# Where the prompt's top-k rounds are written: one block ahead of the mixer loop, or shared out inside it

## The chip, the core and the metric

The kernel runs on one core of a Trainium2 chip. The metric is the device time of one execution in microseconds (us): 992.89 us is the median of three runs of the kernel before (992.37 to 999.76).

## What is computed

One inference step of a decoder layer, for 512 new prompt tokens and for 8 sequences of 4 new tokens each (32 "sample" tokens) that attend to 1024 cached positions in pages. Two attention branches work on the same normalised input:

```
# branch A: an index score picks 256 keys per query, then softmax attention over those
score = einsum('bth,bths->bts', w_i, relu(einsum('bthe,bse->bths', q_i, k_i))) * (IDX_DIM ** -0.5)
_, idx = lax.top_k(where(causal, score, -inf), n_sel)        # n_sel = 128 for the prompt, 256 for the samples
o_a = softmax(q_a . k_a[idx]) @ v_a[idx]
# branch B: stick-breaking attention, exp(log_beta + later) from a reversed cumulative sum
merged = gates[0] * (o_a @ w_br_a) + gates[1] * (o_b @ w_br_b)
h = x + merged @ w_o
y = rmsnorm(h + ffn(rmsnorm(h)))                              # SwiGLU feed-forward, width 2816
```

The new key and value rows are outputs too. All is float32.

## The kernel before

**Matrix products.** A float32 weight is split into a rounded high part (`wh`, on ScalarE, L113) and a low part (`wl`, on GpSimd, L117), the activations likewise (`xh`, `xl`), and each product is three TensorE passes (`xh·wh`, `xh·wl`, `xl·wh`, L502). These passes are most of TensorE's work. They are called dense rows below.

**Stages, in the program's order.** Normalising the input; the index projections (`dense_idx`), then the index scores of prompt and samples (`idx_prompt`, `idx_sample`); the projections of branch B (`dense_qb`, `dense_kb`, `dense_vb`); then the top-k of the prompt; then the mixer loop (`beside`); then merging, the output projection, the feed-forward network and the final norm.

**The two top-k.** `topk_prompt` (L658 to L662) works on three score tiles of 256, 384 and 512 columns, one for each block of 128 queries after the first. For each it makes 16 rounds (L619, L620): VectorE finds the eight largest values of each row, and replaces them by a mark; at the end L662 makes the mask from the marks. That is 48 rounds and three closing instructions, all on VectorE. `topk_sample` (L624 to L657) finds each sample query's 256th largest score by bisection over the 32 bits of a float: per bit VectorE counts the scores above a candidate (L632), TensorE adds the counts of four partition groups by a product with a 128x128 matrix and one column (L635), and VectorE reads that sum and forms the next candidate (L636, then L641; L639 and L643 at the first and last bit). Its scores come by four small transfers of the SP queue (L627). When the bits are done, VectorE makes the mask `mask_s` in seven instructions (L648 to L656).

**The mixer loop.** `beside` draws three generators in turn: `samples` (branch B, then branch A, for the samples), `heads` (branch B for the prompt: L859, L935, L938 to L942, L866, L875; then branch A for the prompt: L859, L972 to L976, L866, L875) and a chain of dense work (gates, branch A's projections, then branch B's output product). Before each draw `topk_share` (L1331) draws from `topk` until `TK_N` times the progress of the stream is reached. The last uses: the prompt's masks are read at L972, the samples' mask at L1145 by a product that starts the sample scores of branch A.

**What sets the order.** The program is built with a scheduler that replays the program in its own timeline and decides each engine's order; the order in which Python emits the instructions is its input and not its result. Each engine then runs its list strictly in turn: an instruction that waits holds back all behind it on that engine.

**Buffers that matter here.** The score products of branch A and B for the prompt (L859) write one pair of PSUM banks, `z`, of which there is a single buffer: the next L859 waits until the last reader of the pair is done (L942 in branch B, L972 in branch A).

Of the kernel before, what the change touches and what calls it, by code (L numbers as in the profile page):

```python
# [279 lines left out]
def chain(gens):  # L280
    for g in gens:
        yield from g
# [3 lines left out]
S_COST = 130  # L286
H_COST = 80
D_COST = 174
TK_N = 80
D_LAT = 6.0  # L290
G_LAT = 8.0
H_LAG = 1
# [7 lines left out]
def hybrid_step(ctx: ExitStack, tc: tile.TileContext, x_prompt, x_sample, cache_kv_a, cache_k_idx, cache_kv_b,  # L300
# [315 lines left out]
    def rounds(w, m, count):  # L616
        for _ in range(count):
            m8 = cpool.tile([P, 8], F32, tag="m8", name="m8", bufs=4)
            nc.vector.max(out=m8[:m], in_=w)  # L619
            nc.vector.match_replace(out=w, in_to_replace=m8[:m], in_values=w, imm_value=TAKEN)  # L620
            yield 0

    def topk_sample():


        for g in range(4):
            nc.sync.dma_start(score4[g * NS:(g + 1) * NS, :], score_s[:, g * part:(g + 1) * part])  # L627
        cand = cpool.tile([P, 1], I32, tag="cand", name="cand", bufs=3)
        nc.gpsimd.memset(cand, 0)
        for bit in range(31, -1, -1):  # L630
            cnt = cpool.tile([P, 1], F16, tag="cnt", name="cnt", bufs=2)
            nc.vector.tensor_scalar(ge4, score4, cand.bitcast(F32), None, op0=OP.is_ge, op1=OP.add, accum_out=cnt)  # L632
            ps = lat()
            ps, flip = ps[:, :1], ps[:, 1:2].bitcast(I32)
            nc.tensor.matmul(ps, group, cnt, start=True, stop=True)  # L635
            nc.vector.tensor_scalar(flip, ps, float(NSEL), -1.0 if bit == 31 else float(1 << bit), op0=OP.is_lt, op1=OP.mult)  # L636
            new = cpool.tile([P, 1], I32, tag="cand", name="cand", bufs=3)
            if bit == 31:
                nc.vector.tensor_scalar(new, flip, 1 << 30, None, op0=OP.bitwise_xor)  # L639
            elif bit:  # L640
                nc.vector.scalar_tensor_tensor(new, flip, 1 << (bit - 1), cand, op0=OP.bitwise_xor, op1=OP.bitwise_xor)  # L641
            else:
                nc.vector.tensor_tensor(new, flip, cand, op=OP.bitwise_xor)  # L643
            cand = new
            yield 0
        least, rank_s = cand[:NS].bitcast(F32), mask_s.bitcast(F16)
        more = cpool.tile([NS, 2], F32, name="more")
        nc.vector.tensor_scalar(tied_s, score_s, least, None, op0=OP.is_equal)  # L648
        nc.vector.tensor_scalar(score_s, score_s, least, None, op0=OP.is_gt, op1=OP.add, accum_out=more[:, 0:1])
        nc.vector.tensor_scalar(more[:, 1:2], more[:, 0:1], -1.0, float(NSEL), op0=OP.mult, op1=OP.add)  # L650
        nc.vector.tensor_tensor_scan(rank_s, tied_s, tied_s, 0.0, OP.add, OP.bypass)
        nc.vector.scalar_tensor_tensor(tied_s, rank_s, more[:, 1:2], tied_s, op0=OP.is_le, op1=OP.mult)
        nc.vector.tensor_add(score_s, score_s, tied_s)
        nc.vector.tensor_scalar(mask_s[:, :PAST].rearrange("q (j k) -> q k j", j=8),
                                score_s[:, :PAST].rearrange("q (k j) -> q k j", j=8), -NEG, NEG, op0=OP.mult, op1=OP.add)
        nc.vector.tensor_scalar(mask_s[:, PAST:], score_s[:, PAST:], -NEG, NEG, op0=OP.mult, op1=OP.add)  # L656
        yield 0  # L657

    def topk_prompt():
        for i in (1, 2, 3):  # L660
            yield from rounds(work_p[i - 1], P, 16)
            nc.vector.tensor_scalar(mask_p[i - 1], work_p[i - 1], -3.2e38, -NEG, op0=OP.is_gt, op1=OP.mult)  # L662
# [582 lines left out]
    V["hp"] = hp  # L1245
    for _ in chain([dense_qb(), dense_kb(), dense_vb()]):
        pass
    for _ in topk_prompt():
        pass
    topk = topk_sample()  # L1250

    V["wide"], V["banks"] = False, cycle([mm, acc])

# [76 lines left out]
    def topk_share(share):  # L1330
        while done[0] < TK_N * share:  # L1331
            next(topk, None)
            done[0] += 1
# [463 lines left out]
```

## Time and profile before

| what | us |
|---|---|
| median of three runs | 992.89 |
| the profiled execution | 993.59 |
| its span, first to last instruction | 991.8 |
| TensorE busy in the span | 936.3 |
| VectorE busy | 642.0 |
| first prompt round (L619) to the last, start | 86.6 to 163.7 |
| first sample bit (L632) to the last, start | 177.8 to 363.9 |
| first use of the samples' mask (L1145) | 404.1 |

The mixer loop runs from about 175 us to 517 us of the span. A row of the profile that names a group gives the line, the engine, the operation, output<-input, shapes and count, then busy time, mean duration in ns, and the idle time of that engine just before with what ended it. A row of the timeline begins with the start and the duration in us; what stands in brackets at its end is the time its engine stood idle before it and what released it. A row of the windows gives the stretch, its length, and for each engine the busy time and the number of instructions, then TensorE's granted clock as a share of full speed, and the DMA share.

### The profile page before, as it was taken

To read this page: it belongs to the slowest core of one execution; us is meant where nothing else is said; L and a number is where in the kernel's file an instruction comes from. 1 tells how busy PE (TensorE), PEld (TensorE's weight loads), DVE (VectorE), ACT (ScalarE), POOL (GpSimd) and SP (SyncE) were. 2 spreads that over 40 slices of the span, in tenths; PEclk is the share of its full clock that TensorE was granted. 3 is DMA by queue.
4 is the path that set the end of the run, shared out by engine and by line. 5 is a ranking of instruction groups with operands and counts; after the bars stand their busy time and mean duration, and the time that the engine had idled before them with its cause. 6 is when DMAs were issued, how large, how long until landed. Compare 5 with 4: busy or idle time off the path is not lost. (4 is left out here: it accounts for less than half of the span.)

```text
span 991.8 us, 19649 instructions
## 1 busy us (share of the span) xinstructions
PE 936.3 (94%) x7412; PEld 846.0 (85%) x7412; DVE 642.0 (65%) x1238; ACT 450.0 (45%) x889; POOL 301.0 (30%) x260
## 2 busy tenths in 40 slices
PE   5989999889898999999989999999999999999995
PEld 4989999756476885778778999989999999999994
DVE  4466998465464657543405576987778788875874
ACT  6224543445244444544565446444444445442453
POOL 3633353211221221313257356122322322201331
PEclk9989999989998999999998999999999999999998
DMA  9773554967786488516376744123333431235212
GB/s 267 188 190 108 142 147 135 296 190 213 241 258 209 135 294 289 178 55 224 110 230 211 215 131 129 44 80 91 87 107 98 115 97 30 67 94 162 81 49 91
DMA packets 180409, 150.67 MB, mean 152 GB/s; under 512 B 12379, under 2 KB 147355, under 8 KB 179291
## 3 DMA queue, kind: packets, MB, share of 16 engines
q1 hardware_dynamic: 175146, 134.45, 45.6%
q0 software_dynamic: 1872, 10.75, 3.0%
q10 hardware_dynamic: 3296, 4.23, 1.4%
q8 instruction: 58, 0.95, 0.4%
q14 instruction: 37, 0.30, 0.1%
HBM read 126.43 MB, written 17.56 MB: 145 GB/s over the span
## 5 line engine op out<-in xcount | busy, mean ns | idle before, releaser
L117 POOL TENSOR_TENSOR wl<-wst,wh 128x512 fp32r<-128x512 f32 (+2 forms) x136 | 161.2, 1207 | 305.7 <-ACT wh L113 298.3
L502 PE MATMUL mm<-xh,wh 128*128 128x256 f32 (+2 forms) x464 | 141.4, 305 | 7.7 <-ACT hT L1381 5.5
L502 PE MATMUL mm<-xl,wh 128*128 128x256 f32 (+2 forms) x464 | 137.9, 297 | 0.1
L502 PE MATMUL mm<-xh,wl 128*128 128x256 f32 (+2 forms) x464 | 136.9, 295 | 0.1
L237 POOL TENSOR_TENSOR wl<-wst,wh 128x512 fp32r<-128x512 f32 (+1 forms) x48 | 68.7, 1453 | 171.9 <-ACT wh L234 156.6
L502 PEld LDWEIGHTS mm<-xh,wh 128*128 128x128 f32 (+1 forms) x464 | 89.3, 192 | 19.0 <-ACT hT L1381 5.7
L113 ACT ACTIVATE wh<-wst 128x1024 fp32r<-128x1024 f32 (+3 forms) x83 | 75.1, 906 | 52.8 <-PE ts L1647 20.5
L502 PEld LDWEIGHTS mm<-xl,wh 128*128 128x128 f32 (+1 forms) x464 | 89.1, 192 | 5.4 <-issue 4.5
L234 ACT ACTIVATE wh<-ws 128x1024 fp32r<-128x1024 f32 (+1 forms) x55 | 54.9, 998 | 80.2 <-PE ffB L1562 29.2
L502 PEld LDWEIGHTS mm<-xh,wl 128*128 128x128 f32 (+1 forms) x464 | 89.1, 192 | 1.9 <-issue 1.4
L239 DVE TENSOR_TENSOR wl<-ws,wh 128x1024 fp32r<-128x1024 f32 (+1 forms) x55 | 66.6, 1211 | 6.2 <-ACT wh L234 6.2
L234 ACT ACTIVATE wh<-wst 128x1024 fp32r<-128x1024 f32 (+1 forms) x34 | 34.8, 1024 | 21.4 <-PE ffB L1562 14.7
L1030 PE MATMUL ts<-ident,kb 128*128 128x128 f32 x256 | 40.0, 286 | 2.3 <-PE ts L1030 0.7
L237 POOL TENSOR_TENSOR wl<-raw,wh 128x384 fp32r<-128x384 f32 x14 | 15.0, 1088 | 79.5 <-ACT wh L234 64.4
L941 DVE TENSOR_TENSOR_SCAN g<-g,z 128x128 f32<-128x128 f32 (+3 forms) x32 | 26.1, 817 | 19.7 <-ACT z L939 16.9
L538 ACT ACTIVATE rowy<-mm 128x256 f32<-128x256 f32 (+1 forms) x40 | 15.7, 393 | 49.0 <-PE mm L502 40.4
L1030 PEld LDWEIGHTS ts<-ident,kb 128*128 128x128 f32 x256 | 29.7, 145 | 9.4 <-ACT kk L843 2.0
L938 ACT ACTIVATE g<-z 128x128 f32<-128x128 f32 (+3 forms) x32 | 13.9, 436 | 49.8 <-PE z L935 35.9
L843 ACT ACTIVATE kk<-ts 128x512 f32<-128x512 f32 x43 | 25.1, 598 | 21.5 <-PE ts L1030 20.9
L1647 PE MATMUL ts<-actp,wh 128*128 128x288 f32 x160 | 34.1, 295 | 0.0
L211 DVE TENSOR_TENSOR ws<-wst 128x1024 f32<-128x1024 f32 (+1 forms) x11 | 19.7, 1790 | 19.6 <-DMA wst<-in_w_ffn_up 19.0
L1740 PE MATMUL dnB<-x,wh 128*128 128x272 f32 x144 | 29.8, 291 | 0.0
(486 smaller groups left out, 3099.2 us busy)
## 6 DMA issues: line engine op xcount, KB each, us to landing
wst<-in_w_in SPq DMA_DIRECT2D x38, 512.0 KB
kb<-in_cache_kv_b SPq DMA_DIRECT2D x64, 256.0 KB
vb<-in_cache_kv_b SPq DMA_DIRECT2D x64, 256.0 KB
wst<-in_w_ffn_gate SPq DMA_DIRECT2D x40, 256.0 KB
wst<-in_w_ffn_up SPq DMA_DIRECT2D x40, 256.0 KB
wst<-in_w_ffn_down SPq DMA_DIRECT2D x16, 320.0 KB
gate_d<-rowy SPq DMA_DIRECT2D x16, 272.0 KB
gt<-gate_d SPq DMA_DIRECT2D x16, 272.0 KB
```

The source lines that it names most:

```text
L113: self.nc.scalar.activation(h, st, AF.Copy)
L117: self.nc.gpsimd.tensor_sub(l[:, k], st[:, k], h[:, k].bitcast(F32))
L211: v.tensor_add(t, a("A21"), a("A22"))
L234: self.nc.scalar.activation(h, src, AF.Copy)
L237: self.nc.gpsimd.tensor_sub(l[:, g], src[:, g], h[:, g].bitcast(F32))
L239: self.nc.vector.tensor_sub(l, src, h.bitcast(F32))
L502: nc.tensor.matmul(ps, ww[:, k, :m], aa[:, k, hs], start=(k == 0 and p == 0), stop=(k == nk - 1 and p == 2))
L843: nc.scalar.activation(dst, ps, AF.Copy)
L941: nc.vector.tensor_tensor_scan(gr, gr, z[:, :n], 1.0, OP.mult, OP.bypass)
L1030: nc.tensor.transpose(tp[:, (2 * j + pg) * P:(2 * j + pg + 1) * P], raws[pg][:, (2 * jj + j) * P:(2 * jj + j + 1) * P], ident)
L1647: nc.tensor.matmul(ps, ww[:, k - ks[0], :], aa[:, hs], start=(k + p == 0), stop=(k + 1 == DOWN[-1][-1] and p == 2))
L1740: nc.tensor.matmul(ps, ww[:, k, :], t[:, i, :], start=(first and k == 0 and p == 0), stop=(k == KQ - 1 and p == 2), skip_group_check=True)
```

## The change

The prompt's rounds are no longer drawn to their end ahead of the loop; they are put in front of the samples' bisection in the generator that the loop draws from, and the number of draws over the loop's progress rises from 80 to 200. The generator now has 48 + 33 draws instead of 33, so that both versions have emitted the last of them at about two fifths of the loop.

```
-TK_N = 80
+TK_N = 200
...
     for _ in chain([dense_qb(), dense_kb(), dense_vb()]):
         pass
-    for _ in topk_prompt():
-        pass
-    topk = topk_sample()
+    topk = chain([topk_prompt(), topk_sample()])
```

No instruction is added or removed: each engine has the same instructions as before. What differs is the order that the scheduler makes of them, and it differs only inside the mixer loop. The first 203 rows of VectorE's list are the same in both versions, and all 96 rows of the prompt's rounds are among them; at the loop's end the last 419 rows are the same again. TensorE's list is the same in its first 1068 and its last 3232 rows.

First place: VectorE at the start of the loop. `g` and `b` are branch B's tiles, L845 is a copy out of PSUM, `ge`, `cnt` and `cand` belong to the samples' bisection. Before:

```order
L620 MATCH_REPLACE work_263<-m_1993,work_263 128x512
L806 TENSOR_TENSOR rlin<-rlin,wrow 32x256
L799 TENSOR_REDUCE sTi<-rli 128x8x4 x2
L662 TENSOR_SCALAR work_263<-work_263 128x512
L807 TENSOR_REDUCE sTi<-rlin 32x32
L817 TENSOR_TENSOR score_s<-tp,masks 32x32
L845 COPY kk<-ts 128x512
L1016 COPY qb<-qsm 64x8x4 x8
L632 TENSOR_SCALAR ge_266,cnt<-score_265,cand 128x264
L1074 TENSOR_TENSOR zr<-acc,masks 128x32
L636 TENSOR_SCALAR tp<-tp 128x1
L941 SCALAR_TENSOR_TENSOR g_2040<-g_2040,z 128x128
```

Now:

```order
L620 MATCH_REPLACE work_263<-m_3606,work_263 128x512
L806 TENSOR_TENSOR rlin<-rlin,wrow 32x256
L799 TENSOR_REDUCE sTi<-rli 128x8x4 x2
L662 TENSOR_SCALAR work_263<-work_263 128x512
L807 TENSOR_REDUCE sTi<-rlin 32x32
L817 TENSOR_TENSOR score_s<-tp,masks 32x32
L845 COPY kk<-ts 128x512
L1016 COPY qb<-qsm 64x8x4 x8
L1074 TENSOR_TENSOR zr<-acc,masks 128x32
L941 SCALAR_TENSOR_TENSOR g_1893<-g_1893,z 128x128
L942 TENSOR_TENSOR b<-z,g_1893 128x128
L845 COPY kk<-ts 128x512
```

The prompt's last round (L620) and closing instruction (L662) stand where they stood; what left this place is the samples' bisection. Its first count (L632) is now 20 rows later, its first sum on TensorE (L635) 435 rows later, in the middle of branch B, and its last sum 257 rows later (row 2109 instead of 1852).

Second place: VectorE at the end of the bisection, where `mask_s` is made; `sm` and `mx` are branch A's softmax tiles for the prompt. Before:

```order
L651 SCALAR_TENSOR_TENSOR mask_s<-tied_s 32x1056
L650 TENSOR_SCALAR more<-more 32x1
L652 SCALAR_TENSOR_TENSOR tied_s<-mask_s,more,tied_s 32x1056
L972 ISA sm,mx<-z,masks 128x128
L972 ISA mx 128x1
L972 ISA sm,mx<-z,masks 128x128
L972 ISA mx 128x1
L1082 SCALAR_TENSOR_TENSOR sbg<-sbg 128x512
L653 TENSOR_TENSOR score_s<-score_s,tied_s 32x1056
L975 RECIPROCAL mx<-mx 128x1
L1084 TENSOR_TENSOR zr<-zr,sbg 128x512
L975 RECIPROCAL mx<-mx 128x1
```

Now:

```order
L651 SCALAR_TENSOR_TENSOR mask_s<-tied_s 32x1056
L975 RECIPROCAL mx<-mx 128x1
L650 TENSOR_SCALAR more<-more 32x1
L972 ISA sm,mx<-z,work_262 128x384
L972 ISA mx 128x1
L976 TENSOR_SCALAR sm<-sm,mx 128x384
L652 SCALAR_TENSOR_TENSOR tied_s<-mask_s,more,tied_s 32x1056
L975 RECIPROCAL mx<-mx 128x1
L653 TENSOR_TENSOR score_s<-score_s,tied_s 32x1056
L976 TENSOR_SCALAR sm<-sm,mx 128x384
L654 TENSOR_SCALAR mask_s<-score_s 32x128x8
L656 TENSOR_SCALAR mask_s<-score_s 32x32
```

The mask was made beside the first block of branch A's softmax; it is now made beside the third.

Third place: TensorE where the sample scores of branch A read the mask. `z<-kaa,qqa` is a prompt score product of branch A, `tp<-ident,sm` transposes its weights, `tp<-pt,va` sums its values, `mm<-...` are dense rows. Before, at the first read of 512 columns:

```order
L502 MATMUL mm<-xh,wh 128x256
L502 MATMUL mm<-xh,wl 128x256
L502 MATMUL mm<-xl,wh 128x256
L866 MATMUL tp<-ident,sm 128x128 x3
L1145 LDWEIGHTS mb
L1145 MATMUL acc<-mask_s,mb 128x512
L866 MATMUL tp<-ident,sm 128x128 x2
L1136 MATMUL ts<-ident,kav 128x128 x8
L866 MATMUL tp<-ident,sm 128x128
L859 MATMUL z<-kaa,qqa 128x128 x2
```

Now:

```order
L859 MATMUL z<-kaa,qqa 128x128 x2
L502 MATMUL mm<-xl,wh 128x256
L875 MATMUL tp<-pt,va 64x256 x2
L875 MATMUL tp<-pt,va 64x128 x2
L502 MATMUL mm<-xh,wh 128x256
L502 MATMUL mm<-xh,wl 128x256
L502 MATMUL mm<-xl,wh 128x256
L866 MATMUL tp<-ident,sm 128x128 x4
L1145 LDWEIGHTS mb
L1145 MATMUL acc<-mask_s,mb 128x512
L1146 MATMUL acc<-kat,qad 32x512 x4
L859 MATMUL z<-kaa,qqa 128x256 x2
```

Before, 24 dense rows stand ahead of those shown, back to the score product before; now three or four stand between two products here. Over the last eight blocks of branch A (two of its four head pairs) 240 dense rows stood between the score products, and now 99. The first of branch A's score products moved 134 rows later in TensorE's list, the last 61, and the first read of the mask 176. From the last sum of the bisection (L635) to that read stand 62 dense rows, 12 transposes (L866) and one pair of 512-column score products. Between rows 1068 and 2678 TensorE changes between dense rows and other work 202 times, before it was 169 times. On the SP queue two of the four L627 transfers now stand 79 rows later, behind the first page loads and the reads of eight more page numbers.

## The prediction

> **What bounds the kernel now.** I read the page first, for the engine that is never free:
>
> ```profile
> PE 936.3 (94%) x7412; PEld 846.0 (85%) x7412; DVE 642.0 (65%) x1238; ACT 450.0 (45%) x889; POOL 301.0 (30%) x260
> PE   5989999889898999999989999999999999999995
> DVE  4466998465464657543405576987778788875874
> ```
>
> TensorE is busy for 936.3 of 991.8 us, and its instructions are the same in both versions, so a gain can only come out of the 55 us in which it stands idle or out of stretches with a lower clock. The prompt's rounds lie in the slices in which VectorE reads 9 and 8, and TensorE reads 9 there too: the rounds hide behind the projections already. Next the windows of the loop, for where the idle time is (stretch, length, then busy time and count of TensorE, its weight loads, VectorE, ScalarE, GpSimd, then TensorE's granted clock, the DMA share and GB/s):
>
> ```profile
> 178.00:300.00 122.00, 111.61 (x913) 79.38 (x914) 67.60 (x179) 53.08 (x122) 23.34 (x18) 0.97 0.77 238
> 300.00:370.00 70.00, 65.50 (x552) 53.00 (x551) 37.77 (x93) 27.95 (x60) 16.88 (x13) 0.95 0.65 207
> 370.00:480.00 110.00, 110.00 (x874) 81.42 (x873) 57.82 (x175) 54.64 (x140) 24.80 (x23) 1.00 0.53 182
> ```
>
> Branch B (178 to 370) has 10.4 + 4.5 = 14.9 us of idle TensorE and a mean clock of 0.97 and 0.95; branch A (370 to 480) has none. So what the change can win lies in branch B, and what it can spoil lies in branch A. Third, TensorE's waits from 174 to 370 us, for what ends the idle time:
>
> ```profile
> PE z L859 <- DVE b L942: 3.9, 2, 3.5
> PE ts L1006 <- DVE zr L1084: 1.9, 2, 1.4
> PE tp L635 <- DVE ge L632: 1.8, 2, 1.3
> PE z L935 <- DVE b L942: 1.8, 2, 1.2
> PE acc L1096 <- DVE zr L845: 1.3, 1, 1.3
> ```
>
> The largest five wait for VectorE, 10.7 us in sum. VectorE has spare time there (67.6 busy of 122), so it is late because its list runs in turn, not because it is full. One thing that holds it is the bisection:
>
> ```profile
> L619 DVE MAX8 m<-work x48: 416/561/696, 86.6 to 163.7; 128x8 f32<-128x256 f32 x16, 128x8 f32<-128x384 f32 x16, 128x8 f32<-128x512 f32 x16
> L636 DVE TENSOR_SCALAR tp<-tp 128x1 int32<-128x1 f32 x32 | 5.2, 162 | 20.0 <-PE tp L635 19.8
> L632 DVE TENSOR_SCALAR_CACHE_REDUCE ge<-score,cand 128x264 uint8<-128x264 f32 x32 | 15.5, 485 | 3.3 <-DMA score<-score_s 2.4
> ```
>
> At L636 VectorE stands for 19.8 us in all until TensorE has come to the one-column product L635, and copies and softmax steps stand behind it. The first row shows the prompt's rounds at 86.6 to 163.7 us, ahead of the loop.
>
> **The change part by part.** *The prompt's rounds.* VectorE's first 203 rows are the same in both versions and hold all of them. The scheduler, given the rounds late, puts them into the same idle places of VectorE. Their price and their cover (the projections, TensorE at 9) stay: 0 us, with no way to either side, since nothing ahead of row 203 differs; without that cover L619 alone would be 48 x 0.56 = 27 us.
>
> *The bisection leaves the first part of branch B.* Its sums move from TensorE's rows 1069 to 1852 to rows 1504 to 2109. What goes with certainty is TensorE's own wait at L635, 1.8 us. Of the waits on `zr` and of those on `b` at L935 (1.9 + 1.3 + 1.8 = 5.0 us) I take half, 2.5 us, since the chains behind them (ScalarE's sigmoids, the scan, the product) remain and the bisection is only a part of their lateness. The wait at L859 is mostly something else:
>
> ```profile
> 299.34 0.72 DVE L555 TENSOR_TENSOR rowy<-rowy,cosT 128x544 f32<-128x544 f32 x1 [4.54 <-DMA roww<-rowy]
> 304.47 0.80 PE L859 MATMUL z<-kk,qq 64*128 64x128 f32 x4 [3.52 <-DVE b L942]
> 208.00:212.00 4.00, 1.75 (x14) 0.92 1.07 344
> 212.00:216.00 4.00, 3.08 (x14) 0.50 0.54 199
> 216.00:220.00 4.00, 3.72 (x25) 0.73 0.00 0
> 304.00:308.00 4.00, 3.53 (x18) 0.50 0.76 248
> ```
>
> VectorE stood for 4.54 us at L555 on a transfer, and TensorE waited behind that; such instructions stay, so I count nothing. The last four rows (stretch, length, TensorE's busy time and count, clock, DMA) show what an idle place costs on top: after 208 to 212 us, with 1.75 us of work in 4, the clock is at 0.50 and then 0.73. That loses 4 x (0.08 + 0.50 + 0.27) = 3.4 us. A second such drop follows the wait at 304. I take half of the first, 1.7 us. The term is -(1.8 + 2.5 + 1.7) = **-6.0 us**. Its ends: 0, if new waits replace all of it, and -(10.7 + 2 x 3.4) = -17.5, if all five waits and both drops go.
>
> The Trainium skill ("TensorE: Matmul & The Clock Gate", Part 1: The HAM clock gate) lets the clock fall to half only after an idle window of about 3.4 us. Here it fell after 2.25 us of idle time in four, spread over more than one wait; so by the rule shorter stalls below would cost only themselves, by the row they may cost 3.4 us more, and I keep that as an end of the range.
>
> *The mask is made later.* Its chain in the old order, VectorE's timeline:
>
> ```profile
> 365.95 0.16 DVE L643 TENSOR_TENSOR cand<-tp,cand 128x1 int32<-128x1 int32 x1
> 366.14 0.76 DVE L648 TENSOR_SCALAR tied_s<-score_s,cand 32x1056 uint8<-32x1056 f32 x1
> 366.93 1.30 DVE L649 TENSOR_SCALAR_CACHE_REDUCE score_s<-score_s,cand 32x1056 f32<-32x1056 f32 x1
> 368.17 3.33 DVE L651 TENSOR_TENSOR_SCAN mask_s<-tied_s 32x1056 f16<-32x1056 uint8 x1
> 371.58 1.30 DVE L652 SCALAR_TENSOR_TENSOR tied_s<-mask_s,more,tied_s 32x1056 uint8<-32x1056 f16 x1
> 374.43 1.22 DVE L653 TENSOR_TENSOR score_s<-score_s,tied_s 32x1056 f32<-32x1056 f32 x1
> 376.31 2.45 DVE L654 TENSOR_SCALAR mask_s<-score_s 32x1024 bf16<-32x1024 f32 x1
> 378.35 0.42 DVE L656 TENSOR_SCALAR mask_s<-score_s 32x32 bf16<-32x32 f32 x1
> L1145 PE MATMUL acc<-mask_s,mb x6: 184/384/385, 404.1 to 478.3; 32*128 32x512 bf16 x4, 32*128 32x32 bf16 x2
> ```
>
> These eight rows take 10.9 us; the mask was ready at 378.8 us and first read at 404.1, 25 us later. Now the chain stands among four softmax instructions of the 384-column block and two reciprocals, and the mask's reader stands close behind. Their prices, and TensorE's for what stands between the last L635 and the first L1145 (62 dense rows, 12 transposes, one 512-column pair):
>
> ```profile
> L972 DVE CUSTOM_DVE_ANT_0 sm<-z,work 128x384 f32<-128x384 f32 x8 | 4.1, 552 | 2.1 <-PE z L859 2.1
> L975 DVE RECIPROCAL mx<-mx 128x1 f32<-128x1 f32 x32 | 5.1, 161 | 6.8 <-ACT sm L974 6.8
> L976 DVE TENSOR_SCALAR sm<-sm,mx 128x384 f32<-128x384 f32 x8 | 4.4, 548 | 0.3
> 75.00:100.00 25.00, 25.00 (x198) 1.00 0.39 112
> 297.45 0.60 PE L866 MATMUL tp<-ident,b 128*128 128x128 f32 x4
> 471.13 1.13 PE L859 MATMUL z<-kaa,qqa 64*128 64x512 f32 x4
> ```
>
> VectorE: 10.9 + 0.2 for L636 + 2 x 0.55 + 2 x 0.55 + 2 x 0.16 = 13.6 us. TensorE: a stretch of nothing but dense rows ran 198 in 25 us, 0.126 us each, so 62 x 0.126 = 7.8, 12 transposes at four in 0.6 us less the overlap, about 0.12 each, 1.4, and the pair 1.1: 10.3 us. TensorE would arrive about 3.3 us early; as its mixture also runs a little slower than back to back, I take **+3.0 us**. Ends: 0, and 3.3 + 3.4 (a clock drop) = 6.7.
>
> *Branch A is pressed together.* Its score products begin 134 rows later and end 61 rows later, and over the last eight blocks 99 dense rows stand between them where 240 did.
>
> ```profile
> L859 PE MATMUL z<-kaa,qqa x64: 272/481/693, 369.8 to 471.7; 64*128 64x128 f32 x16, 64*128 64x256 f32 x16, 64*128 64x384 f32 x16, 64*128 64x512 f32 x16
>   ACT sm L974: 21.7, 13
> ```
>
> Sixteen blocks took 102 us, 6.4 us each. TensorE now has 141 x 0.126 / 8 = 2.2 us less per block: 4.2 us. VectorE needs 57.8 / 16 = 3.6 us per block (the row 370 to 480) and can't run ahead, since the single pair `z` is given back only after both L972, and a reciprocal waits for ScalarE's exponential behind L972 (second row: ScalarE's 21.7 us of waits for L972). With 0.6 us to spare per block I take a quarter of a microsecond for each of eight, **+2.0 us**. Ends: 0, and, if the waits of the rows above are added (6.8 us over 32 reciprocals and 2.1 over 8 L972, two of each in a block: 0.9 us), 4.5 instead of 4.2 us for each of the 12 blocks after the fourth, and one clock drop, 3.6 + 3.4 = 7.0.
>
> *More breaks between dense rows and other work*, 202 against 169:
>
> ```profile
> 298.02 0.36 PE L502 MATMUL mm<-xh,wh 128*128 128x256 f32 x1
> 298.22 0.28 PE L502 MATMUL mm<-xh,wl 128*128 128x256 f32 x1
> 298.34 0.28 PE L502 MATMUL mm<-xl,wh 128*128 128x256 f32 x1
> ```
>
> A first dense row after transposes keeps its follower 0.20 us away, the next 0.12: 0.08 us for each return. Half of 33 changes are returns: **+1.3 us**; ends 0 and 2.6.
>
> *Two score transfers later on SP.* They are issued ahead of VectorE's first count, which stands 20 rows later; 0 us, and at most the 2.4 us that the same count waited for them before.
>
> Sum: -6.0 + 3.0 + 2.0 + 1.3 = +0.3 us on the profiled 993.6, so 993.9. That execution lies 0.7 us above the median of the runs, so against the median I predict **993 us**: no change.
>
> **The rivals**, each worked out on the profiled 993.6. *A: branch B recovers all of it.* The bisection was the thread on which all five waits hung; they go with both drops (-17.5), the mask's 3.0 and the breaks' 1.3 remain: 993.6 - 13.2, 980 us. For it speaks that each wait names VectorE and that VectorE stood 19.8 us at L636; against it that 4.54 us at L555 belong to a transfer. *B: branch A becomes bound by VectorE.* It decides from the point at which a block of softmax, its waits included, takes longer than TensorE's 4.2 us. Then 3.6 us are lost over 12 blocks and 3.4 by a clock drop, the mask costs 3.0 + 3.4, the breaks 1.3, and only L635's 1.8 are won: 993.6 + 12.9, 1006 us. For it speaks the single `z`, against it 0.6 us of slack per block. *C: L555 holds VectorE anyway*, so that only the 1.8 us are won and the losses come as summed: 993.6 + 4.5 = 998 us.
>
> **How the numbers follow.** My forecast, 0.44; A 0.21; B 0.20; C 0.15. A measurement of this kernel can tell about 1% (10 us) from no change. Faster by over 1%: 0.21. Slower: 0.20. Within 1%: 0.59. The likeliest case alone gives 986 to 1000. The range for 8 in 10 reaches to A and to B: 980 to 1006; it leaves out their far sides and what all bounds together would give.
>
> **What would show it.** Right: the prompt's rounds at 86 to 164 us again; less idle TensorE than 10.4 us from 178 to 300; a wait of 2 to 5 us at L1145, or at the L866 just ahead of it, for VectorE; short waits of TensorE for L972 or L976 after 400 us, where there were none. Wrong: no wait at the mask, idle time in branch B as before, or more than 10 us of idle TensorE in branch A.

## The result, and the profile after

The changed kernel takes 1006.5 us (median of 4 runs, 1003.9 to 1007.7); the kernel before took 994.2 us beside it (four runs; the first three had given 992.89). The ratio is 1.0121, 95% interval 1.0084 to 1.0157: slower by 1.2%, where no change was forecast, and half a microsecond beyond the range. The profiled execution of the change, the fastest of its four, took 1003.9 us (span 1001.7), against 993.59 (991.8) before. Its page:

```profile
PE 936.6 (93%) x7412; PEld 847.1 (85%) x7412; DVE 645.7 (64%) x1238; ACT 449.2 (45%) x889; POOL 298.7 (30%) x260
PE   5989999889989997989987999989999999999995
DVE  4466998453565542575613576987778788875874
```

TensorE is busy as long as before (936.6 and 936.3 us). The idle time, span less busy, rose from 55.5 to 65.1 us; that is 9.6 of the 9.9 us by which the span grew. The same windows of the loop as in the prediction (busy time and count of TensorE, weight loads, VectorE, ScalarE, GpSimd, then clock, DMA share, GB/s):

```profile
178.00:300.00 122.00, 108.59 (x881) 79.05 (x882) 61.07 (x104) 51.42 (x118) 23.73 (x18) 0.94 0.76 242
300.00:370.00 70.00, 70.00 (x604) 55.50 (x604) 36.80 (x108) 31.27 (x66) 12.63 (x10) 1.00 0.63 194
370.00:480.00 110.00, 99.25 (x778) 75.71 (x777) 59.22 (x202) 43.91 (x115) 27.18 (x24) 0.95 0.53 184
```

The first part of branch B became worse (13.4 us idle, before 10.4), its second part has no idle time left (before 4.5), and the stretch in which branch A lay, which had none, has 10.8 us. TensorE's waits from 174 to 370 us:

```profile
PE z L935 <- DVE b L942: 4.4, 3, 1.7
PE ts L1030 <- issue: 1.9, 1, 1.9
PE ts L1006 <- DVE zr L1084: 1.6, 1, 1.6
PE ts L1030 <- DVE kk L845: 1.5, 2, 1.3
PE acc L1096 <- DMA vb<-in_cache_kv_b: 1.5, 1, 1.5
PE ts L1030 <- ACT kk L843: 1.1, 1, 1.1
```

The waits at L635, and those at L859 on `b`, are gone; those on `b` at L935 grew from 1.8 to 4.4 us. From 370 to 535 us two waits are new:

```profile
PE acc L1096 <- DMA vb<-in_cache_kv_b: 7.3, 2, 6.3
PE acc L1145 <- DVE mask_s L656: 2.8, 1, 2.8
```

The first is for pages of the samples' values, the second for the samples' mask. The order of events around them, in rows of one instruction each (count, shortest, median, longest, first and last start), of the bisection's sums on TensorE, the mask's last instruction on VectorE and the mask's readers:

```profile
L635 PE MATMUL tp<-cnt,group x32: 167/177/185, 300.6 to 420.1; 128*128 128x1 f16 x32
L656 DVE TENSOR_SCALAR mask_s<-score_s x1: 378/378/378, 434.3 to 434.3; 32x32 bf16<-32x32 f32 x1
L1145 PE MATMUL acc<-mask_s,mb x6: 171/384/385, 434.7 to 494.1; 32*128 32x512 bf16 x4, 32*128 32x32 bf16 x2
L859 PE MATMUL z<-kaa,qqa x64: 272/482/693, 404.4 to 493.6; 64*128 64x128 f32 x16, 64*128 64x256 f32 x16, 64*128 64x384 f32 x16, 64*128 64x512 f32 x16
```

Before, the sums ran from 178.3 to 365.5 us, the mask was ready at 378.8, its readers came at 404.1 and branch A's score products at 369.8. Now the sums begin 122 us later and end 55 us later, and the mask's readers come 31 us later, as soon as the mask is there. Branch A's first keys come later too; SyncE's queue in the change, then in the kernel before:

```profile
382.60 1.49 SPq L412 DMA_DIRECT2D vb<-in_cache_kv_b  x2
384.19 1.35 SPq L1310 DMA_DIRECT2D kaa<-ka_d  x2
```

```profile
357.55 1.34 SPq L1312 DMA_DIRECT2D kaa<-ka_d  x2
391.93 0.33 SPq L412 DMA_DIRECT2D vb<-in_cache_kv_b  x1
```

The load of the keys `kaa` now stands behind the last value page; before, value pages were still issued 34 us after it.

### The profile page after: what moved, and what is told of

Read it like the earlier page. It is cut to its first block, busy times and chain, and to the rows that moved or that the text cites. A ratio compares the mean times of both kernels' runs of the same rounds, so it can differ in the third digit from the quotient of the medians.

```text
span 1001.7 us, 19654 instructions
## 1 busy us (share of the span) xinstructions
PE 936.6 (93%) x7412; PEld 847.1 (85%) x7412; DVE 645.7 (64%) x1238; ACT 449.2 (45%) x889; POOL 298.7 (30%) x260
## 5 line engine op out<-in xcount | busy, mean ns | idle before, releaser
L1030 PE MATMUL ts<-ident,kb 128*128 128x128 f32 x256 | 39.9, 290 | 5.4 <-issue 1.9
L1030 PEld LDWEIGHTS ts<-ident,kb 128*128 128x128 f32 x256 | 31.1, 149 | 9.8 <-issue 3.7
```

The lines of the kernel that those rows point to most:

```text
L1030: nc.tensor.transpose(tp[:, (2 * j + pg) * P:(2 * j + pg + 1) * P], raws[pg][:, (2 * jj + j) * P:(2 * jj + j + 1) * P], ident)
```

## The experiments

Two theories were put against each other. The first, which I held after reading this trace: the later sums hold back branch B's last head pair, so `kaa` comes behind the value pages, the samples' value products stand alone and are starved of pages, 8.7 us of waits in all and a clock drop. It follows the largest new wait. The rival: the mask is late, and that costs far more than the 2.8 us for which TensorE is seen to wait. Each run stands beside runs of the kernel before on the same chip, whose medians were 991.8 to 994.2 us; the chips differ from run to run, so a difference of two times from different chips can be off by those 2.4 us, and the ratios are the better guide.

**Which part of the change acts.** The rounds inside the loop, the sums as early as before:

```diff
-    for _ in topk_prompt():
-        pass
-    topk = topk_sample()
+    topk, rounds_in = topk_sample(), topk_prompt()
...
+        while drawn[0] < 200 * share:
+            next(rounds_in, None)
+            drawn[0] += 1
```

> The prompt's rounds are drawn inside the loop, the samples' 32 bit steps as early as in the kernel before. The main theory (only the later bit steps cost: they hold back branch B's last head pair, so the load of branch A's first keys, kaa, comes behind the value pages on SyncE, and the samples' value products of the second group have no branch A beside them) expects the time before, 990 to 997 us. A theory by which the drawing of the rounds itself costs expects some 1006 us.

Measured: 994.1 us, ratio 1.0003 (0.9975 to 1.0031). And the sums late alone, the rounds in their block:

```diff
-TK_N = 80
+TK_N = 200
...
-    topk = topk_sample()
+    topk = chain([iter([0] * 48), topk_sample()])
```

> The prompt's rounds stand in their block ahead of the loop, as before; the samples' bit steps alone are drawn 48 draws later and 2.5 times as fast, as in the change. If the delay of the bits is all that the change does, this takes the changed kernel's time, 1003 to 1009 us. If the drawing of the rounds costs, it takes about 994 us.

Measured: 1007.8 us, ratio 1.0143 (1.0096 to 1.0189). What acts is the new place of the samples' bisection; drawing the prompt's rounds inside the loop has no effect that the interval (0.3% to either side) can tell from none.

**Early mask, late keys.** One number:

```diff
-TK_N = 80
+TK_N = 200
```

> The kernel before with the samples' bit steps drawn 2.5 times as fast from the same start: the mask is made some 40 us earlier than before, but branch B's last products and kaa's load still come late, with all value pages ahead of it on SyncE. The main theory (late kaa, starved value products) expects about 1001 to 1006 us. The rival by which the lateness of the bits and the mask is what costs (the wait for the mask, the waits of VectorE for the counts, late in the loop) expects 988 to 995 us.

Measured: 988.1 us, ratio 0.9937 (0.9909 to 0.9965), the fastest version here that computes everything. The first theory's own signs are all there, and it is faster than before. TensorE's waits from 170 to 540 us, and the mask's readers:

```profile
PE acc L1096 <- DMA vb<-in_cache_kv_b: 11.2, 5, 5.6
```

```profile
L1145 PE MATMUL acc<-mask_s,mb x6: 184/384/385, 394.1 to 471.2; 32*128 32x512 bf16 x4, 32*128 32x32 bf16 x2
```

It waits 11.2 us for value pages, more than the changed kernel does (8.7 us in the whole loop). The first theory fails on this run.

**Fewer bytes of value pages**, in the change and later in the kernel before:

```diff
-            page(raw, kvb[:, :, v], n, pg, "o s h d -> s (o h d)")
+            if v:
+                page(raw[:, :256], kvb[:, :, v, :4], n, pg, "o s h d -> s (o h d)")
+                raw = raw[:, None, :256].to_broadcast([P, 2, 256])
...
```

> The changed kernel with value pages of which only the first 256 of 512 columns are loaded, each used twice: it leaves out half of the samples' values. The order of the work stays nearly that of the change. The main theory, by which TensorE waits 8.7 us for value pages near 365 to 392 us and then loses its clock, expects these waits to go, and 994 to 998 us. The rival of the late mask expects no more than 2 us less than the change, 1004 to 1007 us.

Measured: 993.7 us, 12.8 us less than the change, as the first theory wanted. Its control:

> The kernel before with value pages of which half is loaded and used twice, as in the run of the change with half the values: it leaves out half of the samples' values. TensorE waits only 0.6 us for value pages in the kernel before. If the 12.8 us that this edit saves in the change are the change's own loss, it saves little here: 990 to 996 us. If fewer bytes help any order of the work, 980 to 986 us.

Measured: 981.8 us, ratio 0.9891 (0.9862 to 0.9919). The edit saves 11.6 us here too, where TensorE waited 0.6 us for value pages. So it helps any order of the work and says nothing for the first theory: with half the bytes in both, the change still costs 993.7 - 981.8 = 11.9 us.

**The late mask's price.** In the change, the product at L1145 reads zeros, and the steps and the mask are made as before:

```diff
+    open_s = cpool.tile([NS, 128], BF16, name="open_s")
+    nc.gpsimd.memset(open_s, 0.0)
...
-            nc.tensor.matmul(z[:, :w], rowsel[:NS, g, :], mask_s[:, cols], ...
+            nc.tensor.matmul(z[:, :w], rowsel[:NS, g, :], (open_s ... ), ...
```

> The changed kernel with a tile of zeros in the place of the samples' mask in the product at L1145: it leaves out the samples' selection, while the bit steps and the mask are still made. If the wait for the mask has a price of its own (2.8 us of wait and 1.5 us of clock behind it), 1001 to 1004 us. If it is only the pages' wait handed on, or if the next wait takes its place, 1005 to 1008 us. The rival by which the late mask is the main cost expects 998 us or less.

Measured: 993.6 us, ratio 1.0006 (0.9976 to 1.0036): 12.9 us less than the change, three times what the wait (2.8 us) and its clock drop (1.7 us, worked out at the end) would give. Its reader row and its waits from 370 to 535 us (the line numbers are 2 higher than in the change):

```profile
L1147 PE MATMUL acc<-open_s,mb x6: 184/384/385, 397.2 to 480.4; 32*128 32x512 bf16 x4, 32*128 32x32 bf16 x2
```

```profile
PE acc L1098 <- DMA vb<-in_cache_kv_b: 7.9, 2, 6.9
PE mm L502 <- ACT hT L1381: 2.8, 1, 2.8
PE ts L1008 <- DVE sr L1173: 2.3, 1, 2.3
```

The wait for value pages is as long as in the change (7.9 and 7.3 us), and the loss is gone all the same. The traces also say where: TensorE's order is the same in both up to 397 us, where the zeros are first read, and the wait for value pages lies in that common part. At its end the run with zeros is 0.3 us ahead, and where the two orders meet again it is 8.5 us ahead (647.0 and 655.5 us). The control, the same edit in the kernel before:

> The kernel before with zeros in the place of the samples' mask at L1145: it leaves out the samples' selection. No wait for the mask is in the kernel before and the order of TensorE's rows keeps these products where they are. If the late mask is what the change pays for, it saves nothing here: 990 to 996 us. If the samples' products without the mask help any order, 980 to 986 us.

Measured: 992.6 us, ratio 1.0000 (0.9976 to 1.0024). The edit saves nothing where the mask was early. Without the mask the change costs 993.6 - 992.6 = 1.0 us; with it, 12 to 13. Taken by the ratios, each to its own chip, the zeros save 1.0121 - 1.0006 of the time before, 11 us, and the two intervals leave some 5 us to either side.

> The changed kernel with both edits: half of each value page, and zeros for the samples' mask; it leaves out half of the samples' values and their selection. Each alone took the change back to some 994 us. If these are two losses of their own, both cures together give 979 to 985 us. If they are one loss (the starved value products hold up the counts and so the mask, or only the samples' blocks that follow matter), 989 to 995 us.

Measured: 985.1 us, ratio 0.9911 (0.9877 to 0.9946). With half the bytes the zeros still save 993.7 - 985.1 = 8.6 us, though TensorE waits there no more than 1.5 us for value pages: the mask's price does not come from the starved pages. The two savings add, though not in full.

**Earlier and later masks in the changed order.** One number of the change, to 160 and to 400 draws:

```diff
-TK_N = 200
+TK_N = 160
```

> The changed kernel with 160 draws a loop in place of 200: the bit steps end later still, but branch A's first keys are loaded ahead of 18 of the value pages, and its blocks lie among the samples' second value products. The main theory (the value products that stand alone are starved: 9.2 us of idle TensorE and lost clock at 345 to 400) expects less than 3 us lost there, a wait for the mask of 3 us or more, and 994 to 1000 us. The rival (the lateness of the bits and the mask is what costs) expects 1006 us or more.

Measured: 1008.9 us, ratio 1.0158 (1.0097 to 1.0218), as the rival wanted. The keys come early (`kaa` issued at 356.3 us), the value pages are waited for less, and the mask comes at 452 us. TensorE's waits from 430 to 535 us:

```profile
PE ts L1006 <- DVE sr L1171: 4.3, 1, 4.3
PE z L859 <- DVE mx L972: 3.3, 3, 1.5
PE mm L502 <- ACT rowy L538: 1.3, 3, 0.6
PE acc L1145 <- DVE mxs L1150: 1.2, 2, 0.8
```

No wait for the mask is among them: the lateness is paid in the softmax of the blocks that read it (`sr` and `mxs`, the samples' softmax tiles) and of the prompt's blocks that share VectorE with them (`mx`). The same kernel with zeros in the mask's place:

> The kernel with 160 draws a loop (1009 us, branch A's keys early, mask made at 451 us), with zeros for the samples' mask; it leaves out the samples' selection. If the late mask is the loss there (16.7 us of idle TensorE after 450 us, for VectorE's sr and mx of the samples' blocks), this takes 15 us or more off: 988 to 994 us. If something else of that order costs, 1002 us or more.

Measured: 987.0 us, ratio 0.9933 (0.9908 to 0.9959), 21.9 us less. Its waits in the same stretch:

```profile
PE mm L502 <- ACT hT L1381: 3.1, 1, 3.1
PE ts L1138 <- ACT kat L845: 1.9, 1, 1.9
PE tp L868 <- DVE sm L978: 0.3, 1, 0.3
```

The waits for `sr`, `mx` and `mxs` went with the mask. They make 8.8 of the 21.9 us; the shorter wait for `hT` (6.1 us, now 3.1) makes another 3.0, and the rest is no single wait. With 400 draws:

> The changed kernel with 400 draws a loop: the bit steps begin and end earlier than in the change, the mask is early, and branch A's first keys are loaded after all value pages, later than in the change. The main theory expects the value pages to be waited for 8 us or more near 360 to 400, no wait for the mask, and 997 to 1003 us; if early bits save elsewhere what the pages cost, as they did where they began at the loop's start, 988 to 992 us. The rival expects 990 to 996 us with no need of the pages to explain it.

Measured: 989.5 us, ratio 0.9969 (0.9942 to 0.9997), inside the second of the first theory's ranges and half a microsecond under the rival's. TensorE waits only 2.0 us for value pages in the whole loop, not 8, though the keys come last: the first theory had that wrong too. Last, a real mask made early by fewer steps, in the change:

```diff
-        for bit in range(31, -1, -1):
+        for bit in range(31, 15, -1):
...
-            elif bit:
+            elif bit > 16:
```

> The changed kernel with the upper 16 of the 32 bit steps alone: it leaves out the lower 16 bits of the threshold. The steps begin as late as in the change, but the real mask is there some 50 us earlier. If the lateness of the mask is the loss, it goes without any zeros in its place: 985 to 995 us. If it is the steps' new place, or the samples' products that run before branch A, 1000 us or more.

Measured: 992.9 us, ratio 1.0008 (0.9981 to 1.0034). Its steps and readers:

```profile
L635 PE MATMUL tp<-cnt,group x16: 167/177/178, 295.6 to 352.7; 128*128 128x1 f16 x16
L1145 PE MATMUL acc<-mask_s,mb x6: 184/384/385, 399.8 to 472.0; 32*128 32x512 bf16 x4, 32*128 32x32 bf16 x2
```

The steps begin as late as in the change, and there is no loss once they end early. This run is support and not proof: VectorE also has less to do (630.3 us busy, 645.7 in the change), branch B is done sooner, the value pages are waited for less, and no run tried 16 steps in the kernel before. In the run with zeros all the steps are done.

Put together, what zeros in the mask's place save goes with the time at which the mask was first read:

| kernel | first read of the mask, us | time, us | with zeros | saved |
|---|---|---|---|---|
| before | 404.1 | 993.4 | 992.6 | 0.8 |
| change, half values | 425.4 | 993.7 | 985.1 | 8.6 |
| change | 434.7 | 1006.5 | 993.6 | 12.9 |
| 160 draws | 453.2 | 1008.9 | 987.0 | 21.9 |

From 425 to 453 us each microsecond of lateness costs (21.9 - 8.6) / 27.8 = 0.48 us; carried back, that line is at nothing near 407 us, close to where the kernel before reads the mask. The intervals leave 4 to 6 us on each of the last three savings, so the slope is a rough one.

**Other places for the early steps**, in the kernel before:

```diff
-TK_N = 80
+TK_N = 120
```

> The kernel before with 120 draws a loop in place of 80: the bit steps end some 40 us earlier, and branch A's first keys are still loaded ahead of 24 value pages. The main theory expects no wait for value pages over 2 us near 345 to 400, none for the mask, the stall of 3.5 us at 301 smaller, and 980 to 988 us, under the 988 us of the faster bits whose pages were starved. If that kernel's gain came from something else than the earlier bits, 990 to 995 us.

Measured: 1003.0 us, ratio 1.0093 (1.0059 to 1.0127), against every expectation (by the medians on that chip it is 11 us): the mask is ready at 329 us and first read at 404.0, the keys are early, and 9 us are lost by the ratio.

> The kernel before with 120 draws a loop (1003 us, though its mask was made 75 us before its first use), with zeros for the mask; it leaves out the samples' selection. By the theory of the late mask this order has no such loss, so its extra 9 us are something else and stay: 1000 to 1005 us. If the mask counts there in a way that the trace does not show, 990 to 995 us.

Measured: 1006.2 us, ratio 1.0151 (1.0101 to 1.0201). The mask has no part in that loss, as the theory says of a kernel whose mask is early.

> The kernel before with 160 draws a loop: the bit steps and the mask early, branch A's first keys loaded ahead of 20 value pages. By the theory of the late mask no loss, and the steps leave branch B's later half as with 200 draws: 985 to 992 us. If 120 draws were slow for a reason that goes with early keys, 1000 us or more.

Measured: 992.3 us, ratio 0.9985 (0.9959 to 1.0010).

> The kernel before with 300 draws a loop: the bit steps faster still, the mask early, branch A's first keys behind all value pages, as with 200 draws (988 us). By the theory of the late mask 984 to 992 us. If each new place of the steps gives a time of its own with no rule, it can lie anywhere from 985 to 1005 us.

Measured: 991.0 us, ratio 0.9972 (0.9943 to 1.0001). Of four settings with early steps, three (160, 200 and 300 draws) lie at 988 to 992 us and one (120) at 1003. An early mask is needed for a good time, not enough for one. What 120 draws lose stays open: no single wait in its trace is as long as the loss.

## Why the prediction was wrong, by its own steps

*The prompt's rounds, 0 us:* right. They run where they did, and the run with the rounds alone inside the loop gave 994.1 us.

```profile
L619 DVE MAX8 m<-work x48: 419/561/696, 87.2 to 164.4; 128x8 f32<-128x256 f32 x16, 128x8 f32<-128x384 f32 x16, 128x8 f32<-128x512 f32 x16
```

*The mask is made later, +3.0 us:* the step that failed. The wait was foreseen, 2.8 us at L1145 where 3.3 were worked out. The mis-sized term is the price: 12.9 us by the run with zeros, less the 0.8 us that the same edit saves before, so 12.1 us (11 by the ratios), beyond the 6.7 us of the term's far end. I priced a late value by the wait of its first reader. Behind that reader stand all the samples' blocks of branch A. The first reader is late by 31 us, and the last value products of those blocks (L1182) still by 13.8 us, before and in the change:

```profile
L1182 PE MATMUL acc<-vanew,pT x16: 267/280/292, 447.2 to 493.7; 32*32 32x128 f32 x16
L1182 PE MATMUL acc<-vanew,pT x16: 267/280/292, 464.5 to 507.5; 32*32 32x128 f32 x16
```

With zeros the last of them starts at 491.6 us. The mask's chain in the change, on VectorE's timeline:

```profile
423.15 3.33 DVE L651 TENSOR_TENSOR_SCAN mask_s<-tied_s 32x1056 f16<-32x1056 uint8 x1
429.82 1.44 DVE L976 TENSOR_SCALAR sm<-sm,mx 128x384 f32<-128x384 f32 x1
431.19 3.49 DVE L654 TENSOR_SCALAR mask_s<-score_s 32x1024 bf16<-32x1024 f32 x1
434.31 0.38 DVE L656 TENSOR_SCALAR mask_s<-score_s 32x32 bf16<-32x32 f32 x1
```

It stands among the softmax's rows, as forecast. Of the 12.9 us the profiled pair (spans 1001.7 and 992.9) shows 8.8, because the change's profiled execution lies 2.6 us under its median and the other 1.4 us over. TensorE idles 4.5 us less with zeros (60.6 against 65.1) and is busy 4.3 us less for the same 7412 products. Of those 4.3 us, 1.7 lie ahead of 397 us, where the order is the same, so they are a difference of two executions and not the mask's work. Of the idle time 2.6 us are the wait for `hT` at the loop's end, 5.4 us in the change and 2.8 with zeros; the kernel before has it too (5.5 us), so with zeros this order gains something that an early mask did not bring. How lateness turns into time beyond the waits is not settled. Nor is the wait parted from the order: with a late mask the scheduler also puts the samples' products elsewhere (first read 176 rows later in TensorE's list), and no run held that order with an early mask.

Two readings behind this term were slightly off. The stretch from 75 to 100 us holds 24 index-score products (L831) beside the dense rows; dense rows of 256 columns follow each other 0.12 us apart, so 62 of them take 7.4 us and not 7.8. And a clock drop was priced at 3.4 us as if TensorE worked all through it, while it was busy for 5.2 of the 6.7 us from 211.4 to 218.1 (2.6 us at half speed).

*The bisection leaves the first part of branch B, -6.0 us:* wrong in place. VectorE still stands for the sums, longer than before (37.0 us against 19.8), only later:

```profile
L636 DVE TENSOR_SCALAR tp<-tp 128x1 int32<-128x1 f32 x32 | 5.2, 163 | 37.1 <-PE tp L635 37.0
```

L635's own 1.8 us went as said. The half of the waits on `zr` and `b` that I counted did not (3.2 + 1.8 = 5.0 us before; 1.6 + 4.4 = 6.0 now), and neither did the first clock drop; L1030 has new waits. What went is the wait at L859 that I had counted at nothing because a transfer at L555 stood behind it, 3.5 us with its clock drop at 304 us. A drop that was not there before came at 286 us, behind a wait of 1.9 us at L1030. Stretches of the change (length, TensorE's busy time and count, clock, DMA share, GB/s):

```profile
212.00:216.00 4.00, 1.94 (x12) 0.78 0.65 235
216.00:220.00 4.00, 4.00 (x21) 0.50 0.00 0
288.00:292.00 4.00, 3.38 (x17) 0.50 0.80 253
432.00:436.00 4.00, 1.26 (x17) 1.00 0.22 66
436.00:440.00 4.00, 4.00 (x22) 0.57 0.04 10
```

*Value pages:* a step that the prediction did not have. Branch A's keys come 27 us later, and the value products wait 7.3 us near 385 us. This and the stall that went at 301 us may be two sides of the same shift; no run parts them. With the mask out of the way, all of the change but the mask comes to +1.0 us (993.6 against 992.6), where the prediction's other terms make -6.0 + 2.0 + 1.3 = -2.7.

*Branch A is pressed together, +2.0 us:* not seen in the change. Its 16 blocks took 90 us (404.4 to 494.3) against 102, and the largest wait of TensorE for VectorE's part of their softmax from 400 to 535 us is

```profile
PE tp L866 <- DVE sm L976: 0.3, 1, 0.3
```

For ScalarE's copies of the transposed weights (L875 for `pt`) it waits 1.2 us in two places. With 160 draws, where the mask is 18 us later still, such waits do come (3.3 us for `mx`).

*More breaks, +1.3 us:* no run tells it apart. *The score transfers, 0 us:* right, the first count waits 1.4 us for them, before 2.4.

*The rivals.* Rival B named 1006 us, the time that came, with a chance of 0.20, but by luck: of its parts only the mask's wait and a clock drop behind it are there, and its core, 3.6 us of softmax by which branch A is bound, is not. Rival A is out, since the first part of branch B idles more than before. Rival C is out, since the wait behind L555 that it held to be fixed went away. Of the signs named for right, the rounds' place and the wait at L1145 came, less idle time from 178 to 300 us did not, and the softmax waits are 0.3 us. Of those for wrong, two came: branch B idles nearly as before (13.4 us of 14.9), and the stretch from 370 to 480 us idles for over 10 us, there mostly for the value pages, which are not the cause of the loss.

## What to carry to other kernels

Price a value that is made later by all of the work that reads it, not by the wait of its first reader: here a wait of 2.8 us stood for 12 us, and at 160 draws no wait for the mask was left to see while zeros in its place saved 22 us. The largest new wait in the trace after is a suspect, and here it was not the cause: cut that dependence in the changed kernel and in the kernel before, and believe it if only the first gets faster. Where a scheduler sets the order, try the neighbouring settings too (here 988 to 1003 us for the same idea), since one setting alone says little about the idea.

## What the runs showed of the hardware

After the wait of 2.8 us for the mask, which ended at 434.7 us (one of 0.3 us stands half a microsecond ahead of it), TensorE's clock stood at half speed for about 3.4 us, and after two waits of 1.6 us each at 210 to 214 us for about 6.8 us. The 0.57 and 0.78 above are means over four microseconds. In the change:

```profile
436.10:439.50 3.40, 3.40 (x17) 0.50 0.02 5
214.30:221.00 6.70, 6.22 (x31) 0.50 0.05 16
```

The first drop cost half of 3.4 us of work, 1.7 us. The Trainium skill ("TensorE: Matmul & The Clock Gate", Part 1: The HAM clock gate) names an idle window of about 3.4 us. Here shorter waits were enough, so the measurement decides.

Half the bytes of the value pages saved 11.6 us in a kernel in which TensorE waited for those pages 0.6 us. The saving stood under other names. In the kernel before with half values, the windows of branch B, TensorE's wait at L859, and the last L555 of that stretch on VectorE (its profiled execution took 977.1 us, 4.8 under its median):

```profile
178.00:300.00 122.00, 114.64 (x950) 81.38 (x949) 71.29 (x184) 54.93 (x126) 24.15 (x18) 0.99 0.69 215
300.00:370.00 70.00, 69.79 (x585) 52.09 (x585) 44.35 (x107) 32.12 (x72) 16.68 (x12) 1.00 0.64 205
```

```profile
PE z L859 <- DVE b L942: 0.6, 2, 0.3
```

```profile
289.56 0.73 DVE L555 TENSOR_TENSOR rowy<-rowy,cosT 128x544 f32<-128x544 f32 x1 [1.13 <-DMA roww<-rowy]
```

Idle TensorE fell from 14.9 to 7.6 us over branch B, and VectorE waited 1.13 us instead of 4.54 for the small transfer at L555. A likely reading, not tested by any run, is that small transfers beside the pages were late on their account while TensorE's waits named VectorE.
